# Seven products in place of eight: the MLP matrices of a hybrid diffusion step by Strassen's scheme

## The chip, the cores and the metric

The kernel runs on one core of a Trainium2 chip. The metric is the time of one execution on the device in microseconds, as the median of several runs; lower is better. On the core, TensorE (PE) multiplies, VectorE (DVE), ScalarE (ACT) and GpSimd (POOL) work elementwise, and SyncE (SP) issues the transfers (DMA) between DRAM and the core's memory.

## The reference

One inference step of a backbone of two layers, with 128 context tokens and 1024 latent tokens of width 1024. Layer 0 mixes the tokens with a gated linear recurrence in both directions, layer 1 with multi-head latent attention. Each mixer is followed by an MLP; both stand behind an RMS norm with a shift and a scale and ahead of a gate, and these six vectors of a layer come from a condition vector by a matrix (adaLN):

```python
def sq_relu_mlp(h, w1, w2):
    a = jax.nn.relu(h @ w1)          # 1024 -> 4096
    return (a * a) @ w2              # 4096 -> 1024
...
    for l in range(DEPTH):           # DEPTH = 2
        sh1, sc1, g1, sh2, sc2, g2 = adaln_params(cond, ada_w[l], ada_b[l])
        h = modulate(rms_norm(x, norm_mix[l]), sh1, sc1)
        x = x + g1[:, None, :] * mixer(h)
        h = modulate(rms_norm(x, norm_mlp[l]), sh2, sc2)
        x = x + g2[:, None, :] * sq_relu_mlp(h, mlp_w1[l], mlp_w2[l])
```

## The kernel before

**Layout.** The 1152 tokens (latent ones first) are the columns of every tile, cut into three chunks of 384 columns; the 1024 features are eight blocks of 128 partitions. X, the residual stream, is three tiles of 128 × 8 × 384 in f32.

**Products.** Each operand is split into a high part (a cast on ACT) and a low part (a subtraction, `split`, L137). `mm3` (L119) multiplies them with three matmuls of 128 × 128 by 384 columns, high by high, high by low and low by high (L121, L124, L125). So a block of 128 outputs over 1024 inner rows and one chunk is 24 matmuls.

**Weights.** They come as a stream of pieces of 128 × 1024, 512 KB each, in the order of their use. `prefetch` (L83) loads the next piece into one of two `raw` buffers (SP), makes the high part on ACT (L94) and the low part on GpSimd (L96; on VectorE in the recurrent stage), three or four pieces ahead of the one in use. After each piece it calls `ada` (L150), as often as `ada_rate` says: an adaLN job loads 128 rows of the adaLN matrix into the same two `raw` buffers and takes two dots of 128 × 1024 on VectorE (`ada_dot`, L143), one for each condition. In MLP 0 there is one job for each piece; all jobs of layer 1 are done there.

**The MLP** (`mlp`, L346) goes through eight groups of 512 of the 4096 inner rows. Up: four blocks, each over all three chunks, with relu and square on ACT (L353, L354) and the split on ACT and VectorE. Down: eight blocks of the output over these 512 rows, each over three chunks; the result goes from PSUM with the gate into X on VectorE (`residual`, L298). Nothing of the hidden values leaves the core. Each MLP has 4,608 matmuls.

**Around it.** `out_proj` (L696) is the product behind the mixer, eight blocks over the three chunks in two halves; the norm of a chunk follows in the generator `norm_mod` (L269): the sum of squares and the root (`rstd`), then PE spreads the result over the partitions (`spread`, L260), then VectorE and ACT scale, shift and split (`modulate`, L276: L284 scales, L288 makes the high part, L289 the low part). `tick` and `later` set at which point of PE's work each step is written. Instructions of each engine run in the order in which the scheduler of the language puts them, which starts from the order of the code; each waits for the data and buffers it needs.

Of the kernel before, what the change touches and what calls it, by code (L numbers as in the profile page):

```python
# [15 lines left out]
D = 1024  # L16
# [34 lines left out]
RG_STREAM = list(dict.fromkeys((_k, _n // 2 * 2 if _k == "g" else _n) for _k, _n, *_ in RG_ORDER))  # L51
ADA_ORDER = [(0, 5)] + [(1, _j) for _j in range(6)]
# [3 lines left out]
class Emit:  # L56
    def __init__(self, nc, tc, ins, outs):
# [6 lines left out]
        self.cap = 1 << 30  # L64
        self.ready = []
# [17 lines left out]
    def prefetch(self, upto):  # L83
# [3 lines left out]
        while self.piece_i < min(upto, self.cap, self.I["wts"].shape[0]):  # L87
            raw = self.wp.tile([128, 1024], F32, tag="raw", name="raw", bufs=2)
            nc.sync.dma_start(raw, self.I["wts"][self.piece_i])
            extra = self.wpx is not None and self.piece_i % 4 == 3  # L90
            pool, n = (self.wpx, 1) if extra else (self.wp, 3)
            hi = pool.tile([128, 1024], F32R, tag="whi", name="whi", bufs=n)
            lo = pool.tile([128, 1024], F32R, tag="wlo", name="wlo", bufs=n)
            nc.scalar.copy(out=hi, in_=raw)  # L94
            eng = nc.vector if self.piece_i < len(RG_STREAM) else nc.gpsimd
            eng.tensor_tensor(out=lo, in0=raw, in1=hi.bitcast(F32), op=ALU.subtract)  # L96
            self.ready.append((hi, lo))
# [4 lines left out]
            self.ada(n)  # L102

# [15 lines left out]
    def mm3(self, ps, w, h, first, last):  # L119
        nc = self.nc  # L120
        mm = nc.tensor.matmul(ps, lhsT=w[0], rhs=h[0], start=first, stop=False)  # L121
        if first and self.pin:
            self.tc.keep_in_program_order(mm)
        nc.tensor.matmul(ps, lhsT=w[0], rhs=h[1], start=False, stop=False)  # L124
        nc.tensor.matmul(ps, lhsT=w[1], rhs=h[0], start=False, stop=last)  # L125
# [143 lines left out]
    def norm_mod(self, c, x, st, l, js, hi, lo):  # L269
        nc = self.nc  # L270
        yield 4.0
        y = self.rstd(st, D)
        yield 5.0
        self.modulate(c, x, self.spread(y), l, js, hi, lo)

    def modulate(self, c, x, r, l, js, hi, lo, ks=range(KT)):  # L276
        for k in ks:
            for a, b, cond in segs(c):
                t = self.cell()[:, :b - a]
                self.scale_part(t, x[:, k, a:b], r[:, a:b], self.mod[:, l, js + 1, cond, k:k + 1])  # L280
                self.shift_part(t, hi[:, k, a:b], lo[:, k, a:b], self.mod[:, l, js, cond, k:k + 1])
# [11 lines left out]
    def cbig(self, dt, name):  # L293
        return self.cpool.tile([128, 8, CH], dt, tag="C", name=name)
# [9 lines left out]
    def group(self, items, rhs, drain, after=None, chunks=range(NCH)):  # L304

        last = {pi: (m, pi) for m, pi, _ in items}
        for c in chunks:
            self.need(c)
            for m, pi, blocks in items:
# [5 lines left out]
                if c == NCH - 1 and (m, pi) == last[pi]:  # L315
# [26 lines left out]
    def dense(self, p0, ms, rhs, drain, after=None):  # L342
        self.group([(m, p0 + i, range(8)) for i, m in enumerate(ms)], rhs, drain, after)


    def mlp(self, p0, l, H, after_acc, after):  # L346
        nc = self.nc
        for g in range(8):
            hid = [self.cbig(F32R, "hid") for _ in range(NCH)]

            def up(m, c, ps):
                r = self.cell()
                nc.scalar.activation(out=r, in_=ps, func=AF.Relu)  # L353
                nc.scalar.activation(out=r, in_=r, func=AF.Square)  # L354
                self.split(hid[c][:, m], hid[c][:, 4 + m], r)

            def down(m, c, ps):
                self.residual(c, m, ps, l, 5)
                if g == 7:
                    after_acc(c, m)  # L360
# [869 lines left out]
```

## Time and profile before

| what | us |
|---|---|
| median of 3 runs | 2831.04 (2830.58 to 2831.68) |
| the profiled execution | 8126.54 |
| its span | 8124.8 |
| busy in it: PE / VectorE / ACT / GpSimd | 8089.1 / 1430.2 / 1188.1 / 458.2 |
| window of MLP 0 in it, 1455 to 4250 | 2795 |
| window of MLP 1 in it, 6060 to 8125 | 2065 |

The profiled execution took 2.87 times as long as the timed ones, at a granted clock of 1.00. In a row of the costliest groups stand line, engine, operation, the tile written and the tiles read, shapes and count, then the busy time of the group in us, the mean of one in ns, and the engine's idle time ahead of them with what ended it. In a row of a line or tile stand the shortest, the median and the longest in ns. In a row of the windows stand start and end, length, busy time and count of PE, PEld (weight loads), VectorE, ACT and GpSimd, the clock, the share of the transfer engines and GB/s. A row of the timeline has the start, the time it took, the engine and the line.

### The profile page before, as it was taken

What the parts mean: (1) busy time and instruction counts of PE and PEld (TensorE: products, weight loads), DVE (VectorE), ACT (ScalarE), POOL (GpSimd) and SP (SyncE); (2) the same over time, 40 slices, a digit from 0 to 9 for tenths busy, and PEclk for the clock granted to TensorE, in tenths of its full rate; (3) what the DMA queues carried; (4) which work ended last, traced back from release to release, by engine and by line L of the source; (5) the groups of instructions that cost most, each with busy time, mean ns of one, the idle gap of its engine ahead of it and who ended that gap; (6) DMA issues with size and microseconds to landing.
All of it is one profiled execution on the core that took longest, in us unless ns stands there. A gap on an engine that the chain in (4) does not pass through costs nothing.

```text
span 8124.8 us, 39857 instructions
## 1 busy us (share of the span) xinstructions
PE 8089.1 (100%) x16123; PEld 6011.4 (74%) x16123; DVE 1430.2 (18%) x2845; ACT 1188.1 (15%) x2194; POOL 458.2 (6%) x232
## 2 busy tenths in 40 slices
PE   9999999999999999999999999999999999999999
PEld 5565567777777777777777788888877777777777
DVE  3312221211111111110012223322121000110002
ACT  2222210100010000101011123333111110001101
POOL 0000000000000000000001100000000000000000
DMA  2000010000000000000001120000100000000000
GB/s 89 29 18 26 26 42 31 13 21 29 29 23 24 21 21 24 26 29 13 11 18 43 37 67 21 24 18 29 69 16 18 13 21 11 21 15 16 19 13 29
DMA packets 75145, 215.49 MB, mean 27 GB/s; under 512 B 7632, under 2 KB 33040, under 8 KB 73296
## 3 DMA queue, kind: packets, MB, share of 16 engines
q1 hardware_dynamic: 74192, 209.79, 7.6%
q0 software_dynamic: 768, 3.15, 0.1%
q8 instruction: 127, 2.08, 0.1%
q14 instruction: 58, 0.48, 0.0%
HBM read 181.80 MB, written 28.48 MB: 26 GB/s over the span
## 4 chain that ended last, share of the span: by engine, by line
PE 100%; DVE 0%; ACT 0%; DMA 0%; issue 0%; SPq 0%; DVEq 0%; ACTq 0%
PE ps L121 28%; PE ps L124 28%; PE ps L125 28%; PE ps L166 3%; PE ps L984 2%; PE ps L928 1%; PE ps L1008 1%; PE ps L1010 1%; PE ps L930 1%; PE ps L931 1%; PE ps L932 1%; PE ps L1009 1%; PE ps L929 1%; PE ps L236 1%; PE ps L910 0%; PE ps L912 0%
## 5 line engine op out<-in xcount | busy, mean ns | idle before, releaser
L121 PE MATMUL ps<-hhi,whi 128*128 128x384 f32 x2088 | 1654.0, 795 | 3.0 <-ACT hhi L288 3.0
L125 PE MATMUL ps<-hhi,wlo 128*128 128x384 f32 x2088 | 1655.4, 793 | 0.0
L124 PE MATMUL ps<-hlo,whi 128*128 128x384 f32 x2088 | 1655.0, 793 | 0.0
L121 PE MATMUL ps<-hid,whi 128*128 128x384 f32 x1536 | 1185.2, 772 | 0.0
L124 PE MATMUL ps<-hid,whi 128*128 128x384 f32 x1536 | 1184.7, 771 | 0.0
L125 PE MATMUL ps<-hid,wlo 128*128 128x384 f32 x1536 | 1184.2, 771 | 0.0
L121 PEld LDWEIGHTS ps<-hhi,whi 128*128 128x128 f32 x2088 | 833.6, 399 | 317.2 <-issue 256.9
L124 PEld LDWEIGHTS ps<-hlo,whi 128*128 128x128 f32 x2088 | 830.8, 398 | 308.1 <-issue 255.3
L125 PEld LDWEIGHTS ps<-hhi,wlo 128*128 128x128 f32 x2088 | 837.6, 401 | 291.0 <-issue 241.0
L96 POOL TENSOR_TENSOR wlo<-raw,whi 128x1024 fp32r<-128x1024 f32 x161 | 392.1, 2435 | 6733.3 <-ACT whi L94 6733.3
L121 PEld LDWEIGHTS ps<-hid,whi 128*128 128x128 f32 x1536 | 601.9, 392 | 200.2 <-issue 166.1
L125 PEld LDWEIGHTS ps<-hid,wlo 128*128 128x128 f32 x1536 | 599.3, 390 | 203.6 <-issue 169.0
L124 PEld LDWEIGHTS ps<-hid,whi 128*128 128x128 f32 x1536 | 598.1, 389 | 200.0 <-issue 165.7
L298 DVE SCALAR_TENSOR_TENSOR X<-ps,mod,X 128x256 f32<-128x256 f32 (+1 forms) x576 | 285.9, 515 | 2577.1 <-PE ps L125 2558.2
L94 ACT CAST whi<-raw 128x1024 fp32r<-128x1024 f32 x181 | 189.0, 1045 | 3028.8 <-PE ps L124 3028.8
L140 DVE TENSOR_TENSOR hid<-cell,hid 128x384 fp32r<-128x384 f32 x192 | 139.3, 727 | 1979.3 <-ACT hid L139 1979.3
L353 ACT ACTIVATE cell<-ps 128x384 f32<-128x384 f32 x192 | 94.0, 490 | 1575.5 <-PE ps L125 1575.5
L984 PE MATMUL ps<-ident,p 128*128 128x128 f32 x584 | 216.1, 534 | 2.3 <-ACT p L969 2.3
L933 DVE TENSOR_REDUCE mx<-ps 128x1 f32<-128x384 f32 (+1 forms) x200 | 109.4, 547 | 424.3 <-PE ps L932 424.1
L928 PE MATMUL ps<-k,q 128*128 128x384 f32 (+1 forms) x200 | 171.9, 861 | 0.0
L121 PE MATMUL ps<-zhi,whi 128*128 128x384 f32 x192 | 171.5, 893 | 0.0
L125 PE MATMUL ps<-zhi,wlo 128*128 128x384 f32 x192 | 170.7, 889 | 0.0
(189 smaller groups left out, 6554.7 us busy)
## 6 DMA issues: line engine op xcount, KB each, us to landing
raw<-wts SPq DMA_DIRECT2D x181, 512.0 KB, 3.3
raw<-ada_wt SPq DMA_DIRECT2D x56, 512.0 KB, 3.3
adaw<-ada_n SPq DMA_DIRECT2D x24, 512.0 KB, 3.3
o_d<-o SPq DMA_DIRECT2D x64, 128.0 KB, 1.7
x<-xt SPq DMA_DIRECT2D x3, 1536.0 KB, 13.7
X<-xt SPq DMA_DIRECT2D x3, 1536.0 KB, 8.6
xmid<-X SPq DMA_DIRECT2D x3, 1536.0 KB, 5.7
qn_d<-qn SPq DMA_DIRECT2D x6, 768.0 KB, 3.9
```

What stands on the lines that cost most here:

```text
L94: nc.scalar.copy(out=hi, in_=raw)
L96: eng.tensor_tensor(out=lo, in0=raw, in1=hi.bitcast(F32), op=ALU.subtract)
L121: mm = nc.tensor.matmul(ps, lhsT=w[0], rhs=h[0], start=first, stop=False)
L124: nc.tensor.matmul(ps, lhsT=w[0], rhs=h[1], start=False, stop=False)
L125: nc.tensor.matmul(ps, lhsT=w[1], rhs=h[0], start=False, stop=last)
L140: (lo_eng or nc.vector).tensor_tensor(out=lo, in0=src, in1=hi.bitcast(F32), op=ALU.subtract)
L166: self.nc.tensor.matmul(ps[i][0:2], lhsT=self.cs[:, :, k], rhs=w[:, i * 512:(i + 1) * 512], start=(k == 0), stop=(k == 7))
L298: self.nc.vector.scalar_tensor_tensor(out=self.X[c][:, m, a:b], in0=ps[:, a:b], scalar=self.mod[:, l, j, cond, m:m + 1], in1=self.X[c][:, ...
L353: nc.scalar.activation(out=r, in_=ps, func=AF.Relu)
L928: nc.tensor.matmul(ps, lhsT=qh, rhs=kh[:, a:b], start=True, stop=False)
L933: nc.vector.tensor_reduce(out=mx[:, j:j + 1], in_=ps, axis=AX.X, op=ALU.max)
L984: nc.tensor.transpose(ps[:, j * 128:(j + 1) * 128], p[:, (t * 3 + j) * 128:(t * 3 + j + 1) * 128], self.ident)
```

## The change

In both MLPs the products over chunks 0 and 1 follow Strassen's scheme in the form with few sums. The two chunks are the two column halves of the activations and the two halves of the inner rows their row halves (A11, A12 of chunk 0, A21, A22 of chunk 1); blocks m and m + 2 of the output are the two halves of the weights. In place of eight products of a quarter there are seven, and sums of quarters on both sides. Chunk 2 is multiplied as before. The three matmuls of each product stay. Two up blocks over chunks 0 and 1 had 8 × 12 = 96 matmuls and have 7 × 12 = 84; over chunk 2 they keep 48, of which 24 stand in the pair (108) and 24 in a filler, below. An MLP has 4,224 in place of 4,608.

- **Order of the MLP.** Up and down are no longer interleaved by groups: the whole up matrix comes first, then the whole down matrix. The hidden values of 4096 rows don't fit in the core, so they go to DRAM (`hid_d`, nine tiles of 128 × 2 × 384 per group, sums of quarters among them) and come back.
- **Output product and sums.** The second half of `out_proj` takes the chunks in the order 2, 0, 1. X goes to DRAM (`xs_d`), `modulate` with `keep` writes the modulated values of chunks 0 and 1 over X as well, without the split of the first four blocks of chunk 1, which no product uses. `sums` makes S1 to S4 in place on VectorE, each 1536 columns wide, and splits them.
- **Filler.** 16 of the 32 up blocks over chunk 2 are plain pieces of 24 matmuls: `filler(0, 8)` stands between the output product and the up loop, `filler(8, 8)` between up and down loop.
- **Up loop.** 16 pairs. `prep` loads both weight blocks of the next pair into tiles that lie where X was, splits R0 and half of R1 (low part on GpSimd in layer 0, on VectorE in layer 1), makes four sums of 512 columns and splits the two results on VectorE. The products of a pair give h11, h12, h22 and, in `tail`, h21; sums in `st` cells go to DRAM (`put`). Each pair calls `ada` with two or three jobs.
- **Between.** X is loaded again, hidden values are loaded, then comes the second filler with one adaLN job for each piece.
- **Down loop.** 16 steps d of 132 matmuls (84 in the last two): GpSimd makes two splits and four sums of 256 columns for each raw weight, two raw weights a step; nine hidden tiles a group are loaded and split; the results are added to X by `residual`. The last 96 matmuls are chunk 2 over the last group.
- **Pools.** The nine buffers of one pool become six (tag C) and three (tag G).

The core of the diff:

```diff
+    def sums(self, H):
+        q = [self.X[c][:, 4 * i:4 * i + 4] for c in range(2) for i in range(2)]
+        a11, a12, a21, a22 = q
...
+        sub(a22, a21, a22, ALU.add)
+        sub(a21, a11, a21)
+        sub(a11, a22, a11)
+        sub(a12, a12, a11)
+        for i, t in ((1, a11), (0, a22), (2, a21), (3, a12)):
+            self.split(*S[i], t)
...
+        def put(m, slot, t):
+            nc.sync.dma_start(hid_d[m // 4][:, slot, m % 2], t)
...
+        def drain2(m, c, ps):
+            t = self.cell(tag="acc")
+            relu2(t, ps)
+            put(m, 5, t)
...
+        filler(0, 8)
+        for c in range(NCH):
+            self.need(c)
+        self.release(self.xp)
+        self.upx = self.alloc(name="upx", bufs=1, side="right", reuse_waits="tile")
...
+        leng = nc.vector if l else nc.gpsimd
...
+            if part == 0:
+                r = [self.raw(up_row(i), self.upx, 4) for i in (m, m + 2)]
+                W[p] = {"r": r, "R0": self.wsplit(r[0], leng)}
...
+            if part == 1:
+                w["R1"] = self.wsplit(r1[:, b], leng, 512)
+                add(r0[:, a], r1[:, a], r0[:, a], ALU.subtract)
+                add(r1[:, a], r1[:, b], r1[:, a], ALU.subtract)
+                add(r1[:, b], r1[:, b], r0[:, a], ALU.subtract)
+                add(r0[:, b], r0[:, b], r1[:, b], ALU.subtract)
+            else:
+                w["TY"] = self.wsplit(r1, nc.vector)
+                w["TX"] = self.wsplit(r0, nc.vector)
...
+            A = self.bank()
+            self.prod(A, w["R0"], 0, A11, 4, True)
+            s1 = self.cell()
+            nc.scalar.copy(out=s1, in_=A)
...
+            prep(p + 1, 0)
+            B = self.bank()
+            self.prod(B, w["R0"], 4, A12, 4, True)
+            h11 = st()
+            add(h11, B, s1)
+            nc.scalar.activation(out=h11, in_=h11, func=AF.Relu)
+            square(h11)
+            put(m, 1, h11)
...
+            self.ada(3 if p % 2 else 2)
+        tail()
...
+        load(4)
+        for c in range(NCH):
+            x = self.xp.tile([128, 8, CH], F32, tag="X", name="X")
+            nc.sync.dma_start(x, self.xs_d[l][c])
+            self.X.append(x)
+        load(12)
+        self.ada_rate = 1.0
+        filler(8, 8)
+        self.ada_rate = 0.0
+        self.ada(len(self.ada_jobs))
...
+                    b11, b21, b12, b22 = (raw[:, i * 256:(i + 1) * 256] for i in range(4))
+                    sub = lambda out, x, y: nc.gpsimd.tensor_tensor(out=out, in0=x, in1=y, op=ALU.subtract)
+                    sub(b11, b12, b11)
+                    sub(b12, b22, b12)
+                    sub(b22, b22, b11)
+                    sub(b21, b21, b22)
+                V.append(self.wsplit(raw, nc.gpsimd))
...
+            hi, lo = H2[c] = self.hpair2((2, 0, 1).index(c))
+            self.nc.sync.dma_start(self.xs_d[l][c], self.X[c])
...
-        self.dense(pi + 4, range(4, 8), rhs, drain, after)
-        self.ada_rate = 1.0
+        self.dense(pi + 4, range(4, 8), rhs, drain, after, chunks=(2, 0, 1), last_c=1)
```

How the scheduler places this is seen in the order of the engines' instructions. A row has the line, the operation, the tile written and the tiles read, and the shape.

VectorE in MLP 0 before, in the second group: `hid` are hidden values, `raw` adaLN weights, `mod` their results, `X` the residual stream.

```order
L140 TENSOR_TENSOR hid_4751<-cell_5017,hid_4751 128x384
L145 SCALAR_TENSOR_TENSOR junk_2955,mod_73<-raw_5068,cb_2952 128x1024
L145 SCALAR_TENSOR_TENSOR raw_5068,mod_73<-raw_5068,cb_2952 128x1024
L140 TENSOR_TENSOR hid_4751<-cell_5057,hid_4751 128x384
L140 TENSOR_TENSOR hid_4751<-cell_5097,hid_4751 128x384
L145 SCALAR_TENSOR_TENSOR junk_2955,mod_73<-raw_5108,cb_2952 128x1024
L145 SCALAR_TENSOR_TENSOR raw_5108,mod_73<-raw_5108,cb_2952 128x1024
L140 TENSOR_TENSOR hid_4751<-cell_5137,hid_4751 128x384
L298 SCALAR_TENSOR_TENSOR X_2962<-ps_5152,mod_73,X_2962 128x384
```

VectorE in the up loop of MLP 0 now, in the second pair: `raw_4468` and `raw_4470` are the weights of the next pair, the other `raw` are adaLN weights, `st` the hidden values, `wlo` the low parts of the weight sums.

```order
L170 SCALAR_TENSOR_TENSOR junk_2955,mod_73<-raw_4978,cb_2952 128x1024
L170 SCALAR_TENSOR_TENSOR raw_4978,mod_73<-raw_4978,cb_2952 128x1024
L170 SCALAR_TENSOR_TENSOR junk_2955,mod_73<-raw_4982,cb_2952 128x1024
L170 SCALAR_TENSOR_TENSOR raw_4982,mod_73<-raw_4982,cb_2952 128x1024
L446 TENSOR_TENSOR raw_4470<-raw_4470,raw_4468 128x512
L446 TENSOR_TENSOR raw_4468<-raw_4468,raw_4470 128x512
L446 TENSOR_TENSOR st_4572<-ps_4427,cell_4534 128x384
L170 SCALAR_TENSOR_TENSOR junk_2955,mod_73<-raw_5161,cb_2952 128x1024
L165 TENSOR_TENSOR wlo_4595<-raw_4470,whi_4594 128x1024
L446 TENSOR_TENSOR st_4589<-ps_4521,cell_4519 128x384
L165 TENSOR_TENSOR wlo_4599<-raw_4468,whi_4598 128x1024
L170 SCALAR_TENSOR_TENSOR raw_5161,mod_73<-raw_5161,cb_2952 128x1024
```

The dots stood one job to a piece, which is 72 matmuls of PE; now, in pairs 1 to 8, four jobs, eight dots, stand in a pair of 108, among the sums and splits that PE waits for. The code asks for two or three jobs a pair; the scheduler puts them this early, and in pairs 9 to 15 there are none.

SP in MLP 0 before, with pieces and adaLN weights by turns:

```order
L89 DMA raw_5022<-wts 128x1024
L154 DMA raw_5028<-ada_wt 128x1024
L89 DMA raw_5062<-wts 128x1024
L154 DMA raw_5068<-ada_wt 128x1024
L89 DMA raw_5102<-wts 128x1024
```

SP now at the start of MLP 0: `acc` are results of the filler on their way to DRAM, `raw_4246` and `raw_4248` the first up weights.

```order
L415 DMA hid0_2<-acc_4180 128x384
L415 DMA hid0_3<-acc_4209 128x384
L179 DMA raw_4602<-ada_wt 128x1024
L415 DMA hid0_3<-acc_4238 128x384
L111 DMA raw_4246<-wts 128x1024
L111 DMA raw_4248<-wts 128x1024
```

The first up weights are issued behind the store of the filler's last result; their tile lies where X was.

SP now between the two matrices of MLP 0: `acc_7309` is the first result of the second filler, `raw_7313` the third of its eight weights.

```order
L415 DMA hid0_4<-acc_7309 128x384
L563 DMA X_7250<-xs0 128x3072
L563 DMA X_7252<-xs0 128x3072
L563 DMA X_7254<-xs0 128x3072
L111 DMA raw_7313<-wts 128x1024
L179 DMA raw_7319<-ada_wt 128x1024
L415 DMA hid0_4<-acc_7368 128x384
L111 DMA raw_7323<-wts 128x1024
L179 DMA raw_7329<-ada_wt 128x1024
L111 DMA raw_7333<-wts 128x1024
```

Weights and adaLN weights go by turns as before, with the three loads of X and the stores of the filler among them, while a piece is now 24 matmuls of PE.

More of the change, by code (lines that the diff above doesn't have):

```diff
@@ L86, in prefetch @@
             upto = min(upto, len(RG_STREAM) + 3)
[L87 to L94, printed above, removed]
+        while self.piece_i < min(upto, self.cap, len(STREAM)):
+            raw = self.raw(STREAM[self.piece_i])
             eng = nc.vector if self.piece_i < len(RG_STREAM) else nc.gpsimd
-            eng.tensor_tensor(out=lo, in0=raw, in1=hi.bitcast(F32), op=ALU.subtract)
-            self.ready.append((hi, lo))
+            self.ready.append(self.wsplit(raw, eng))
             self.piece_i += 1
@@ L102, in prefetch, with raw, wslot, wsplit @@
             self.ada(n)
+    def raw(self, row, pool=None, n=2):
+        t = (pool or self.wp).tile([128, 1024], F32, tag="raw", name="raw", bufs=n)
+        self.nc.sync.dma_start(t, self.I["wts"][row])
+        return t
+    def wslot(self):
+        kind = self.wcycle[self.wi % len(self.wcycle)]
+        self.wi += 1
+        if kind == "c":
+            t = self.cbig(F32R, "wc", "G").rearrange("p a b -> p (a b)")
+            return t[:, :1024], t[:, 1024:2048]
+        pool, n = {"wp": (self.wp, 3), "x": (self.wpx, 1), "u": (self.upx, 1)}[kind]
+        return tuple(pool.tile([128, 1024], F32R, tag=t, name=t, bufs=n) for t in ("whi", "wlo"))
+    def wsplit(self, raw, eng, n=1024):
+        hi, lo = (t[:, :n] for t in self.wslot())
+        self.split(hi, lo, raw, eng)
+        return hi, lo
     def piece(self, i):
@@ L279, in modulate @@
                 t = self.cell()[:, :b - a]
+                sh = self.mod[:, l, js, cond, k:k + 1]
                 self.scale_part(t, x[:, k, a:b], r[:, a:b], self.mod[:, l, js + 1, cond, k:k + 1])
-                self.shift_part(t, hi[:, k, a:b], lo[:, k, a:b], self.mod[:, l, js, cond, k:k + 1])
+                if not (keep and c == 1 and k < 4):
+                    self.shift_part(t, hi[:, k, a:b], lo[:, k, a:b], sh)
+                if keep and c < 2:
+                    self.nc.scalar.activation(out=x[:, k, a:b], in_=t, func=AF.Identity, bias=sh, scale=1.0)
     def scale_part(self, out, x, r, sc):
@@ L291, in shift_part, with cbig, hpair2 @@
         )
-    def cbig(self, dt, name):
-        return self.cpool.tile([128, 8, CH], dt, tag="C", name=name)
+    def cbig(self, dt, name, tag="C"):
+        return self.cpool.tile([128, 8, CH], dt, tag=tag, name=name, bufs=6 if tag == "C" else 3)
+    def hpair2(self, i):
+        return tuple(self.cbig(F32R, n, t) for n, t in zip(("hhi", "hlo"), ("GG", "GC", "CC")[i]))
     def residual(self, c, m, ps, l, j):
@@ L301, in residual, with group @@
             )
-    def group(self, items, rhs, drain, after=None, chunks=range(NCH)):
+    def group(self, items, rhs, drain, after=None, chunks=range(NCH), last_c=NCH - 1):
         last = {pi: (m, pi) for m, pi, _ in items}
@@ L314, in group @@
                 drain(m, c, ps)
[L315 removed]
+                if c == last_c and (m, pi) == last[pi]:
                     self.done(pi)
@@ L340, in need, with dense @@
                 self.advance(e)
-    def dense(self, p0, ms, rhs, drain, after=None):
-        self.group([(m, p0 + i, range(8)) for i, m in enumerate(ms)], rhs, drain, after)
-    def mlp(self, p0, l, H, after_acc, after):
-        nc = self.nc
[L348 to L360, printed above, removed]
-            self.dense(p0, range(4), lambda k, c: (H[c][0][:, k], H[c][1][:, k]), up)
-            p0 += 4
-            self.ada_until(l, 5)
-            self.group(
-                [(m, p0 + m // 2, [(m % 2) * 4 + k for k in range(4)]) for m in range(8)],
-                lambda k, c: (hid[c][:, k], hid[c][:, 4 + k]), down, after if g == 7 else None,
-            )
-            p0 += 4
-        return p0
+    def dense(self, p0, ms, rhs, drain, after=None, **kw):
+        self.group([(m, p0 + i, range(8)) for i, m in enumerate(ms)], rhs, drain, after, **kw)
@@ L697, in out_proj @@
         sts = [{} for _ in range(NCH)]
-        H2 = []
+        H2 = {}
+        self.cap = pi + 16
         def drain(m, c, ps):
             self.residual(c, m, ps, l, j)
-            self.sq_acc(sts[c], self.X[c][:, m], m)
+            for i in range(m + 1) if m == 4 and c < 2 else [m] if m > 4 or c == 2 else []:
+                self.sq_acc(sts[c], self.X[c][:, i], i)
             if l == 0 and m < 4 and c > 0:
```

244 lines of the change are left out of this document (226 added, 18 removed).

## The prediction

> **What bounds the kernel now.** The page's busy times were read first, then the windows of each stage, then the lines and forms of VectorE, GpSimd and the transfers.
>
> ```profile
> span 8124.8 us, 39857 instructions
> PE 8089.1 (100%) x16123; PEld 6011.4 (74%) x16123; DVE 1430.2 (18%) x2845; ACT 1188.1 (15%) x2194; POOL 458.2 (6%) x232
> L353 ACT ACTIVATE cell<-ps 128x384 f32<-128x384 f32 x192 | 94.0, 490 | 1575.5 <-PE ps L125 1575.5
> ```
>
> PE is busy for the whole profiled span; the others are nearly idle, and ACT, before it takes a result of the up product, waits for PE (1575.5 us). The windows are, in turn, the recurrent stage, its output product, MLP 0, attention, its output product and MLP 1; the columns are span, then PE, PEld, DVE, ACT and POOL busy with counts, the clock, DMA share, GB/s:
>
> ```profile
> 0.00:1140.00 1140.00, 1120.94 (x1643) 670.56 (x1644) 308.40 (x441) 256.11 (x363) 13.11 (x12) 1.00 0.10 37
> 1140.00:1455.00 315.00, 315.00 (x517) 226.51 (x516) 51.53 (x86) 20.31 (x30) 20.02 (x10) 1.00 0.10 34
> 1455.00:4250.00 2795.00, 2795.00 (x4622) 2005.41 (x4621) 371.21 (x659) 234.63 (x403) 166.92 (x70) 1.00 0.06 22
> 4250.00:5780.00 1530.00, 1525.47 (x4090) 1278.74 (x4089) 414.37 (x1091) 423.27 (x962) 85.12 (x60) 1.00 0.10 34
> 5780.00:6060.00 280.00, 280.00 (x640) 220.18 (x640) 49.81 (x99) 30.59 (x51) 25.20 (x14) 1.00 0.14 51
> 6060.00:8125.00 2065.00, 2052.65 (x4619) 1610.04 (x4617) 234.92 (x469) 223.17 (x386) 147.81 (x66) 1.00 0.05 17
> ```
>
> The profiled execution took 8126.54 us, 1.7 us more than its span; the timed runs took 2831.04 us, 2.87 times less. PE alone is stretched: the two MLPs have the same matmuls and show 2795 and 2065 us, together more than the timed kernel. So PE durations of this trace can't be used; VectorE, ACT, GpSimd and transfer durations fit into 2831 us as they are. The sum therefore runs against 2831, and every slack of those engines must be measured against a much faster PE than the page shows.
>
> **The price of a matmul.** All matmuls of the MLPs have 384 columns. If all windows shrink alike, the MLPs are (2795 + 2065) / 8126.54 of 2831.04 = 1693 us, over 9,241 records 0.183 us. If the recurrent stage and attention can't go below VectorE and ACT one after the other (308 + 256, 414 + 423 = 1402), the four PE-bound windows share 1429 us over 10,398 records: 0.137. If those two stages go down to their busier engine (308 + 423 = 731), it is 0.202. I take the middle of the ends, 0.17, and keep both. A product of 12 matmuls is then 2.0 us, a pair of up blocks (108) 18.4, a plain piece (24) 4.1, a filler of eight pieces 32.6, a down step (132) 22.4.
>
> **What is removed.** Per MLP 4,608 matmuls become 4,224: 768 fewer in all, **−131 us** (−105 to −155) as long as PE stays fed. Everything else the change does is to feed it.
>
> **Prices of the feeding.**
>
> ```profile
> L96 POOL TENSOR_TENSOR wlo<-raw,whi x161: 2341/2362/3398, 1033.5 to 7971.9; 128x1024 fp32r<-128x1024 f32 x161
> L96 DVE TENSOR_TENSOR wlo<-raw,whi x20: 1216/1225/1227, 21.2 to 1010.1; 128x1024 fp32r<-128x1024 f32 x20
> L140 DVE TENSOR_TENSOR hid<-cell,hid x192: 545/558/1347, 1524.6 to 7977.2; 128x384 fp32r<-128x384 f32 x192
> L298 DVE SCALAR_TENSOR_TENSOR X<-ps,mod,X x576: 334/545/620, 1157.0 to 8108.5; 128x384 f32<-128x384 f32 x94, 128x128 f32<-128x128 f32 x50, 128x256 f32<-128x256 f32 x48
> L145 DVE SCALAR_TENSOR_TENSOR junk<-raw,cb x56: 1211/1217/3316, 1216.6 to 3647.8; 128x1024 bf16<-128x1024 f32 x56
> L145 DVE DVE_READ_ACCUMULATOR raw<-raw,cb x56: 76/82/85, 1219.0 to 3660.9; 128x1 f32 x56
> L284 DVE SCALAR_TENSOR_TENSOR cell<-X,mod,ps 128x384 f32<-128x384 f32 x48 | 27.6, 605 | 21.4 <-PE ps L264 21.2
> L289 DVE SCALAR_TENSOR_TENSOR hlo<-cell,mod,hhi 128x384 fp32r<-128x384 f32 x64 | 44.8, 738 | 45.9 <-ACT hhi L288 45.9
> L562 DVE SCALAR_TENSOR_TENSOR ti<-ti,xf 128x1152 f32<-128x1152 f32 x16 | 21.7, 1357 | 176.2 <-ACT ti L552 176.2
> L94 ACT CAST whi<-raw 128x1024 fp32r<-128x1024 f32 x181 | 189.0, 1045 | 3028.8 <-PE ps L124 3028.8
> L354 ACT ACTIVATE cell<-cell 128x384 f32<-128x384 f32 x192 | 100.3, 523 | 5.8
> L228 POOL TENSOR_TENSOR acc<-acc,cell x33: 992/1002/2377, 10.4 to 8099.0; 128x384 f32<-128x384 f32 x33
> raw<-wts SPq DMA_DIRECT2D x181, 512.0 KB, 3.3
> 1131.65 0.33 SPq L89 DMA_DIRECT2D raw<-wts  x1
> 1132.50 11.08 SPq L374 DMA_DIRECT2D X<-xt  x3
> ```
>
> VectorE takes 558 ns for 384 columns and 1357 for 1152, some 1.04 ns a column: 0.69 us for 512 columns, 1.75 for 1536. A weight is at hand 0.33 + 3.3 + 1.05 + 2.36 = 7.0 us after its buffer came free: issue, transfer, ACT, GpSimd.
>
> **Start of each MLP, +36.** The first up weights lie on the place of the old X, so their transfer waits for the last split of the operand sums. The spread of chunk 1's norm stands behind five filler pieces on PE (20.4), then come the modulation (8 × 0.605 + 4 × 0.738 + 0.6 of ACT = 8.4), four sums and four splits of 1536 (8 × 1.75 = 14.0), in layer 0 two dots among them (2.4), then the weight, 7.0: 52.2 against the filler's 32.6, so PE waits 19.6. In layer 1 there are no dots and VectorE makes the low half (1.23): 16.
>
> **Up loop, +33 in layer 0, 0 in layer 1.** Each pair asks VectorE for four weight sums (2.8), two splits (2.45), three sums out of PSUM (1.6), four of SBUF (2.2) and, in eight pairs of layer 0 where the order packs the adaLN dots, eight dots at 1.30 (10.4): 19.5 us against PE's 18.4. Two rows of the timeline bear on it:
>
> ```profile
> 1680.07 2.91 POOL L96 TENSOR_TENSOR wlo<-raw,whi 128x1024 fp32r<-128x1024 f32 x1 [14.58 <-ACT whi L94]
> 1680.81 3.25 DVE L145 SCALAR_TENSOR_TENSOR raw<-raw,cb 128x1024 f32<-128x1024 f32 x1
> ```
>
> A dot that takes 1.22 alone took 3.25 and ended 1.1 us after GpSimd's split: it stood still while that ran. The residual, out of PSUM, never exceeds 0.62. In layer 0 GpSimd makes 2.36 + 1.3 us of splits per pair, now beside a VectorE that is never idle: up to 23.2 a pair. Over eight pairs (19.5 to 23.2 − 18.4) × 8 = 9 to 38; I take 22.5 a pair, since only the PSUM sums fit beside GpSimd: 33. The Trainium skill ("SBUF — State Buffer", Who interferes with whom) states this as a rule, one exclusive lock for the port pair of VectorE and GpSimd; the trace agrees (3.25 us for 1.22), and by it the term is 38, without it 9. In layer 1, with no dots and GpSimd's splits on VectorE (1.9), it has 11 us of work per pair, so nothing.
>
> **Between the matrices, +61.** SP is one queue. In layer 0 the reload of X (three transfers that hold SP for 11.1 us) stands behind the store of the filler's first result (PE 4.1, ACT 0.49 + 0.52, issue 0.33) and ahead of the third filler weight: ready at 5.4 + 11.1 + 6.7 = 23.2 us, due at 8.2. Then each weight waits until GpSimd has finished the one before, since the adaLN weights hold the other raw buffer: 7.0 apiece against 4.1. The eighth is ready at 23.2 + 5 × 7.0 = 58.2 and done at 62.3, against 32.6: 30. The first down weight stands behind the last two dots (2.6), loses some 9, its second half behind four GpSimd sums (1.00 for 384 and 2.36 for 1024, so 0.73 for 256) and two splits some 7 more: 46. In layer 1 nothing but X and the store delays the third weight: 15 (23.2 − 8.2).
>
> **Down phase, +8** (0 to 30). At 14 group boundaries the loads of hidden values wait for PE to free a tile, 0.6 each. In a step of 22.4 us GpSimd has four splits and eight sums (4 × 2.36 + 8 × 0.73 = 15.3), VectorE 18 residuals (9.8) and 4.5 splits of 768 columns (0.96 each), so 14, 17 with small ones: both are covered. If that cover goes, every microsecond costs 32 over both layers.
>
> **At nothing:** eight new stores a pair and nine loads in two steps (SP 0.33 us each), since the windows show 0.05 to 0.10 of the transfer engines busy; ACT, with 13 cell passes (6.6) and 3.5 weight casts (3.7) in a pair of 18.4; the chunk order 2, 0, 1 of the output product, which moves work among stretches where PE has all it needs; the three stores of X a layer, ahead of the filler's on SP but behind no load that is due; the last norm, which follows chunk 2's last matmul as before. If SP or ACT lose that cover, a pair shows it on PE at once, 32 times.
>
> Sum: −131 + 36 + 33 + 61 + 8 = +7, so 2838 us. The ends are wide: the gain alone moves by 26 and 24, and the stalls move against it, as a slower PE hides more.
>
> The Trainium skill ("TensorE: Matmul & The Clock Gate", What's actually happening) has the array at half clock after an idle window of some 3.4 us, for as long again; every row above shows clock 1.00, and no run here has such a gap. By an estimate from that page, six gaps would add about 10 us, to 2848.
>
> **Rivals.**
> - *PE is slower than I price it* (0.20 a matmul, near the upper end). The gain is then 154, a pair takes 21.6 and hides most of VectorE's 22.5 (7 left of 33), the start costs 17 + 14 = 31, the middle 25 + 16 + 14 = 55, boundaries 8: −154 + 101 = −53, 2778 us. For it: the page has PE at 100%, and shrinking all windows alike gives 0.183. Against it: the recurrent stage has little PE work, so its window should shrink less. It decides from about 0.174 on, where the terms cancel.
> - *The lock costs little*, as VectorE falls back on PSUM sums and GpSimd runs in its gaps: up loop 9 in place of 33, 2814 us. For it: the split in the row lost 0.55 itself (2.91 against 2.36), so VectorE got part of its work done beside it. Against it: the next dot stood for the rest, and VectorE now leaves no gaps there.
> - *GpSimd becomes the bound of the down phase.* Its 12 instructions a step have 7.1 us of slack; if each waits 0.75 us for VectorE (a 384-wide one takes 0.56, a 768-wide 0.96), a step takes 15.3 + 9 = 24.3, 32 steps lose 1.9 each: 2838 + 61 = 2899 us. It decides from 0.6 us each. For it: the sum of 992 ns once took 2377. Against it: half of VectorE's work there comes out of PSUM.
>
> **How the numbers follow.** A measurement of this kernel tells about 0.2%, 5.7 us, from no change. Forecast, 2805 to 2880 around 2838: 0.42, of it 0.09 faster, 0.08 same, 0.25 slower. Slow PE, around 2778: 0.19. Little lock, around 2814: 0.16, of it 0.12 faster, 0.04 same. GpSimd, around 2899 and above: 0.19. Unforeseen waits: 0.04 slower. Faster 0.40, same 0.12, slower 0.48. The range leaves out the far third of the slow-PE case (0.06), the upper half of the GpSimd case and what is unforeseen (0.14): 2755 to 2900; the likeliest case alone spans 2805 to 2880.
>
> **What the next profile shows.** Right, if 768 matmuls are gone, if PE idles 16 to 20 us before the first pair of each MLP on the weight sums' chain, if VectorE is busy without a gap through eight pairs of MLP 0 with dots of 2 to 3 us, and if the filler between the matrices waits for weights in MLP 0 more than in MLP 1. If PE is as stretched there as here, these gaps shrink in the profile and only the timed runs and single changes can tell. Wrong, if the time falls below 2755 (the stalls are not there, or a matmul costs 0.2), or if steps of the down phase wait for GpSimd or hidden values.

## The result and the profile after

The changed kernel took 3056.95 us (median of 4 runs, 3054.89 to 3061.66) against 2830.81 before: a ratio of 1.0802 (95% interval 1.0783 to 1.0820). The side was right, slower, and the size was not: 226 us lost where 7 were forecast, outside the range of 2755 to 2900.

The profile of the changed kernel is not stretched, and another profiled execution of the kernel before (the first experiment) is not either, so PE can be read in both. The page of the changed kernel:

```profile
span 3059.9 us, 40925 instructions
PE 2716.5 (89%) x15355; PEld 2619.7 (86%) x15355; DVE 1934.0 (63%) x3445; ACT 1376.1 (45%) x2442; POOL 860.9 (28%) x560
```

768 records of PE are gone, and PE is idle for 343 us of the span; in the second profile of the kernel before it is idle for 84. The windows below cut the MLPs of the changed kernel by counting matmuls: first filler (192), up loop (1,728), second filler (192), down loop (2,112), for MLP 0 and then for MLP 1; a gap between two stages counts to the later one. The column behind POOL's count is the granted clock, then come the share of the transfer engines and GB/s.

```profile
478.40:523.80 45.40, 38.90 (x211) 37.78 (x210) 37.62 (x72) 28.86 (x55) 15.14 (x7) 0.89 0.44 139
523.80:863.20 339.40, 310.54 (x1730) 304.86 (x1729) 262.97 (x368) 161.89 (x281) 69.61 (x34) 0.96 0.58 185
863.20:938.30 75.10, 39.55 (x194) 36.15 (x193) 40.17 (x55) 20.66 (x32) 15.83 (x7) 0.80 0.71 241
938.30:1433.90 495.60, 411.63 (x2144) 404.19 (x2144) 287.55 (x461) 132.57 (x158) 292.92 (x205) 0.89 0.30 99
2146.20:2190.60 44.40, 37.62 (x211) 36.68 (x211) 37.90 (x68) 30.18 (x56) 15.10 (x7) 0.92 0.43 138
2190.60:2508.10 317.50, 304.49 (x1731) 303.74 (x1730) 172.53 (x245) 164.17 (x280) 3.04 (x2) 0.98 0.41 137
2508.10:2563.90 55.80, 37.30 (x193) 36.15 (x192) 14.48 (x14) 23.11 (x35) 23.63 (x13) 0.82 0.69 245
2563.90:3045.00 481.10, 405.52 (x2145) 399.44 (x2143) 283.63 (x460) 125.45 (x151) 278.67 (x197) 0.91 0.28 94
```

The two MLPs of the kernel before, in its second profile:

```profile
473.80:1296.60 822.80, 811.76 (x4657) 810.42 (x4656) 383.82 (x698) 242.08 (x415) 160.83 (x71) 1.00 0.23 77
1998.50:2814.10 815.60, 810.66 (x4659) 809.91 (x4657) 249.69 (x483) 231.28 (x400) 152.40 (x67) 1.00 0.13 43
```

In both kernels a matmul of 384 columns starts every 0.173 to 0.175 us when nothing holds it (0.174 is the median over the changed kernel's 12,936). With 0.174 the kernel before has 802 us of matmuls in each MLP and loses 21 and 14. What the changed kernel loses against 0.174 per matmul, by stage, is this:

| stage | MLP 0 | MLP 1 | both | forecast |
|---|---|---|---|---|
| first filler (33.4 of matmuls) | 12 | 11 | 23 | as before |
| up loop (300.7) | 39 | 17 | 56 | 36 + 33 |
| second filler (33.4) | 42 | 22 | 64 | 61 |
| down loop (367.5) | 128 | 114 | 242 | 8 |

The gain is 768 × 0.174 = 134 us. All losses together are 384 against 35 before, so the MLPs are 216 us longer; the other 15 us of the 231 between the spans lie in the stages around them and were not followed up. Three rows of four are near the forecast. The down loop is not.

### The profile page after: what moved, and what is told of

It reads as the page before. It is cut to its first block, busy times and chain, and to the rows that moved or that the text cites. A ratio compares the mean times of both kernels' runs of the same rounds, so it can differ in the third digit from the quotient of the medians.

```text
span 3059.9 us, 40925 instructions
## 1 busy us (share of the span) xinstructions
PE 2716.5 (89%) x15355; PEld 2619.7 (86%) x15355; DVE 1934.0 (63%) x3445; ACT 1376.1 (45%) x2442; POOL 860.9 (28%) x560
## 4 chain that ended last, share of the span: by engine, by line
PE 44%; POOL 7%; issue 6%; DVE 5%; DMA 4%; ACT 2%; SPq 1%; POOLq 0%; DVEq 0%; ACTq 0%
PE ps L146 11%; PE ps L149 11%; PE ps L150 11%; POOL wlo L165 2%; POOL raw L582 2%; DMA hid<-hid 2%; PE ps L1290 2%; POOL wc L165 2%; PE ps L1234 1%; DMA raw<-wts 1%; PE ps L1238 1%; PE ps L1315 1%; PE ps L1237 1%; PE ps L1236 1%; PE ps L1316 1%
## 5 line engine op out<-in xcount | busy, mean ns | idle before, releaser
L332 DVE SCALAR_TENSOR_TENSOR X<-ps,mod,X 128x384 f32<-128x384 f32 (+2 forms) x768 | 392.2, 537 | 395.5 <-PE ps L150 349.9
L146 PE MATMUL ps<-hhi,whi 128*128 128x384 f32 x1576 | 539.3, 344 | 88.6 <-ACT whi L164 71.5
L150 PE MATMUL ps<-hhi,wlo 128*128 128x384 f32 x1576 | 537.7, 341 | 12.3 <-POOL wlo L165 12.3
L149 PE MATMUL ps<-hlo,whi 128*128 128x384 f32 x1576 | 538.0, 342 | 5.5 <-DVE hlo L319 5.5
L146 PEld LDWEIGHTS ps<-hhi,whi 128*128 128x128 f32 x1576 | 301.9, 192 | 104.5 <-ACT whi L164 73.8
L146 PE MATMUL ps<-hid,whi 128*128 128x384 f32 x824 | 294.4, 357 | 72.1 <-DVE X L332 70.1
L150 PEld LDWEIGHTS ps<-hhi,wlo 128*128 128x128 f32 x1576 | 302.3, 192 | 16.5 <-POOL wlo L165 15.8
L149 PEld LDWEIGHTS ps<-hlo,whi 128*128 128x128 f32 x1576 | 302.7, 192 | 11.9 <-DVE hlo L319 6.6
L150 PE MATMUL ps<-hid,wlo 128*128 128x384 f32 x824 | 291.5, 354 | 3.2 <-POOL wlo L165 3.2
L149 PE MATMUL ps<-hid,whi 128*128 128x384 f32 x824 | 291.6, 354 | 0.0
L146 PE MATMUL ps<-hid,wc 128*128 128x384 f32 x584 | 209.5, 359 | 74.7 <-DVE X L332 68.0
L146 PEld LDWEIGHTS ps<-hid,whi 128*128 128x128 f32 x824 | 167.1, 203 | 77.5 <-DVE X L332 44.0
L150 PE MATMUL ps<-hid,wc 128*128 128x384 f32 x584 | 206.0, 353 | 1.1 <-POOL wc L165 1.1
L149 PE MATMUL ps<-hid,wc 128*128 128x384 f32 x584 | 206.6, 354 | 0.0
```

The lines of the kernel that those rows point to most:

```text
L332: self.nc.vector.scalar_tensor_tensor(out=self.X[c][:, m, a:b], in0=ps[:, a:b], scalar=self.mod[:, l, j, cond, m:m + 1], in1=self.X[c][:, ...
```

## The down loop: what PE waits for there

Who waited for whom in the down loop of MLP 0 of the changed kernel (in total, times, longest), first PE, then SP:

```profile
PE ps L146 <- DVE X L332: 68.3, 15, 6.9
```
```profile
SPq L111 <- POOL wlo L165: 212.0, 24, 21.3
SPq L111 <- POOL wc L165: 155.4, 14, 19.3
SPq L555 <- PE ps L150: 58.7, 23, 12.8
```

PE waits for VectorE's residuals (L332), 4.6 us at a time in the mean, though VectorE is busy for only 288 of the 496 us. SP stands for 367 of 496 us ahead of weight loads (L111), until GpSimd has made the last split of an earlier weight and so freed its buffer. The loads of the hidden tiles (L555) are in the same queue. One such wait, from the timeline of the changed kernel (start, duration, engine, line):

```profile
1099.35 10.65 SPq L111 DMA_DIRECT2D raw<-wts  x2
...
1107.25 2.40 POOL L165 TENSOR_TENSOR wlo<-raw,whi 128x1024 fp32r<-128x1024 f32 x1
...
1110.11 0.85 SPq L555 DMA_DIRECT2D hid<-hid  x2
1114.38 1.70 ACT L164 CAST hid<-hid 128x768 fp32r<-128x768 f32 x2 [8.37 <-DMA hid<-hid]
1115.24 0.96 DVE L165 TENSOR_TENSOR hid<-hid 128x768 fp32r<-128x768 f32 x1 [5.13 <-ACT hid L164]
1116.12 0.61 DVE L332 SCALAR_TENSOR_TENSOR X<-ps,mod,X 128x384 f32<-128x384 f32 x1
1116.78 0.69 PE L146 MATMUL ps<-hid,whi 128*128 128x384 f32 x1 [3.17 <-DVE X L332]
1117.27 0.52 PE L149 MATMUL ps<-hid,whi 128*128 128x384 f32 x1
1117.59 0.52 PE L150 MATMUL ps<-hid,wlo 128*128 128x384 f32 x1
...
1119.83 0.41 PE L146 MATMUL ps<-hid,wc 128*128 128x384 f32 x1
1120.08 0.34 PE L149 MATMUL ps<-hid,wc 128*128 128x384 f32 x1
1120.25 0.33 PE L150 MATMUL ps<-hid,wc 128*128 128x384 f32 x1
```

SP sits on the second weight load until GpSimd's split ends (1109.65). Only then go two hidden tiles out (1110.11). ACT casts them 4.3 us later, VectorE, which takes its instructions in order, has stood 5.1 us at their low part, and the residual behind it comes at 1116.12. That residual frees the bank that PE adds to next. Then PE's own rows: behind the gap a matmul starts every 0.32 us (1117.27, 1117.59) for some 3 us, and every 0.17 after that (1120.08, 1120.25). The windows view of the slow stretch has a granted clock of 0.50 (behind the counts):

```profile
1116.78:1119.80 3.02, 3.02 (x9) 3.02 (x10) 3.02 (x6) 0.00 (x0) 0.00 (x0) 0.50 0.00 0
```

So each gap costs itself and a second stretch at half clock.

## The experiments

The theory (A) was this queue: hidden loads stand on SP behind weight loads that wait for GpSimd. Its main rival (B) was the prediction's own: GpSimd is too slow for a step of the down loop. A third (C): PE frees the hidden tiles too late, whoever loads them. Experiments 1 to 11 are one execution each; executions of the changed kernel differ by up to 7 us and those of experiment 12 by 11, so small differences of the total decide little.

**1. The kernel before, again.** No edit.

> The kernel before, unchanged, for a profile that isn't stretched. In the changed kernel a 384-column matmul starts every 0.174 us at full clock, and 5 to 6% of the matmuls start every 0.32 us right behind a gap. Theory A (the slow matmuls are new, made by the new gaps): the kernel before shows under 10 us of such loss in its two MLPs, and each MLP takes 802 to 820 us. Theory B (they are in every kernel): the loss per MLP is like the changed kernel's, some 35 us. Time 2831 either way.

2831.02 us, windows as shown above: 823 and 816 us at clock 1.00, with 21 and 19 matmuls at half clock in the two MLPs (2.6 and 2.3 us lost), against 75 us in the changed kernel's, 59 of them in the down loops. A of this experiment holds, though MLP 0 is 3 us above the 820 that it named: the half-clock matmuls are new and come from the new gaps.

**2. Down weights loaded from GpSimd's queue.**

```diff
-                    raw = D["raw"] = self.raw(base + (n // 8) * 8 + 4 + n // 2 % 4)
+                    raw = D["raw"] = self.raw(base + (n // 8) * 8 + 4 + n // 2 % 4, eng=nc.gpsimd)
```

> The loads of the down weights are issued by GpSimd in place of SP. Theory A (SP is blocked: hidden loads stand behind weight loads that wait for GpSimd's splits to free a buffer): SP's waits for GpSimd in the down loops go, the hidden loads are issued early, PE's gaps in the two down loops fall from 162 us together to under 60 and the slow matmuls behind them from 55 to under 25: 2920 to 2960 us. Theory B (GpSimd itself is too slow for a step): no gain, as GpSimd has the same work and the issues besides: 3050 to 3090. Theory C (the hidden tiles are freed too late by PE): 3020 to 3057.

2989.03 us. The two down loops:

```profile
934.50:1394.90 460.40, 401.01 (x2145) 393.48 (x2144) 294.39 (x458) 132.06 (x157) 313.92 (x237) 0.92 0.33 107
2525.10:2972.00 446.90, 395.98 (x2145) 389.96 (x2143) 294.18 (x460) 126.43 (x153) 299.34 (x227) 0.94 0.31 101
```

35 and 34 us less, while GpSimd is busier than before (314 against 293 us): B falls, since GpSimd did more and the loop went faster. But the time lies between A's range and C's, and the gain is about half of what A expected. The waits of SP and PE in the loop of MLP 0:

```profile
SPq L555 <- PE ps L150: 364.3, 30, 44.0
SPq L111 <- POOL wc L165: 22.6, 2, 14.6
SPq L111 <- POOL wlo L165: 21.3, 6, 7.6
```
```profile
PE ps L146 <- DVE X L332: 39.4, 12, 6.1
```

SP waits 44 us for GpSimd in place of 367, but the hidden loads now wait, one behind the other, for PE to free their tiles (eight of them take SP 19.78 us from 1093.91 on), so a piece of C is in it, and VectorE took 4.74 us for two hidden splits beside GpSimd's (0.96 each alone).

**3. Hidden tiles loaded from ACT's queue.**

```diff
-                nc.sync.dma_start(lo.bitcast(F32), hid_d[i // 9][:, i % 9])
+                nc.scalar.dma_start(lo.bitcast(F32), hid_d[i // 9][:, i % 9])
```

> The loads of the hidden values are issued by ACT in place of SP. Theory A (SP blocked): they no longer stand behind SP's waits for GpSimd, but ACT now waits for PE to free their tiles, with casts behind it; gaps of the down loops from 162 us to 60 to 110: 2950 to 3010 us. Theory B (GpSimd too slow): 3050 or more. Theory C (tiles freed too late): 3040 or more.

2906.46 us, better than any of the three expected. The down loops, and the waits in that of MLP 0:

```profile
933.20:1348.80 415.60, 387.82 (x2144) 383.20 (x2143) 273.45 (x456) 132.80 (x157) 291.61 (x205) 0.95 0.37 117
2484.10:2889.10 405.00, 382.28 (x2145) 378.97 (x2143) 273.21 (x460) 127.54 (x152) 280.87 (x201) 0.97 0.35 111
```
```profile
SPq L111 <- POOL wlo L165: 225.5, 24, 19.3
SPq L111 <- POOL wc L165: 149.7, 14, 13.9
```
```profile
PE ps L146 <- DVE X L332: 13.7, 5, 4.2
```

One word in one line, and the loops lose 80 and 76 us. SP waits for GpSimd as long as ever (375 us), and now no hidden load is behind it; PE's wait for the residuals falls from 68.3 to 13.7. With experiment 2 this shows A: the place in the queue held the loads back. It does not show that A alone is worth the 80 us, for with this edit the scheduler also places VectorE's hidden splits otherwise. Of the 60 in MLP 0's loop, 20 follow directly on another one in the changed kernel, 16 in experiment 2 and 6 here, so that fewer residuals stand behind two of them. No run parts the two.

**4. The four GpSimd sums left out.**

```diff
-                    sub(b11, b12, b11)
-                    sub(b12, b22, b12)
-                    sub(b22, b22, b11)
-                    sub(b21, b21, b22)
```

> The four sums of down weights on GpSimd are left out (256 instructions of 0.74 us in all, so the down products use wrong weights). Theory A (SP blocked behind GpSimd): a weight buffer comes free 2.9 us earlier, 5.9 us a step of 30 us; part of the gaps goes: 2960 to 3010 us. Theory B (GpSimd too slow): its work a step falls from 15.3 to 9.4 us and nearly all gaps of the down loops go: 2860 to 2920. Theory C (tiles freed too late): 3040 or more.

2953.33 us; 7 us under A's range and 33 above B's. The down loops took 443.9 and 431.1 us, 52 and 50 less: GpSimd lost some 110 us of work in each (183 and 167 busy) and PE got less than half of it back. B falls here too: if GpSimd's work bounded the loop, nearly all of it would have come back.

The remaining runs go on from the third, one stall at a time.

**5. The first pair's weights in the ordinary buffers.**

```diff
-                r = [self.raw(up_row(i), self.upx, 4) for i in (m, m + 2)]
+                r = [self.raw(up_row(i), *((self.upx, 4) if p else ())) for i in (m, m + 2)]
```

> On top of the third experiment (2906 us): the first pair's two weights of each up loop are loaded into the two ordinary raw buffers, not into the tiles that lie where X was. Theory A (they wait for the operand sums, which hold X's place): PE's gaps of 15.9 and 13.0 us ahead of the up loops fall under 6 each, with the half-clock matmuls behind them: 2878 to 2890 us. Theory B (the operands S1 to S4 come too late as well, or the ordinary buffers come free no earlier): 2900 to 2908.

2891.54 us: the up loops go from 338.4 to 333.0 and from 317.6 to 309.1. That is 1.5 us above A's range. PE's wait ahead of the first pair is gone, so it was there for the reason given, but 10 of the 15.7 us come back inside the loop of MLP 0, and 4.5 of the 13.0 in MLP 1, where PE now waits for the weight sums.

**6. The up loop's splits on VectorE in layer 0.**

```diff
-        leng = nc.vector if l else nc.gpsimd
+        leng = nc.vector
```

> On top of the third experiment (2906 us): in layer 0 VectorE, not GpSimd, makes the low parts of R0 and R1 in the up loop. Theory A (GpSimd's split stops VectorE for its whole length): VectorE goes from up to 23.2 us a pair to 21.4 and gains up to 1.8 us in each of eight pairs: 2890 to 2904. Theory B (no such stop): it goes from 19.5 to 21.4 and PE loses 1.9 more in each of eight pairs: 2915 to 2925.

2882.56 us. The up loop of MLP 0 in the third experiment, and here:

```profile
518.10:856.50 338.40, 308.84 (x1729) 302.91 (x1728) 263.25 (x367) 161.94 (x281) 70.89 (x34) 0.97 0.58 185
```
```profile
518.10:838.80 320.70, 304.75 (x1729) 304.01 (x1728) 255.62 (x399) 163.46 (x281) 4.33 (x2) 0.97 0.60 195
```

VectorE took over 32 splits and is busy for 8 us less: beside GpSimd its instructions stand still and count as busy. The loop is 18 us shorter, and beyond the start stall only some 4 us of loss are left in it. A holds, 7 us beyond its range. The second to the eighth pair of the changed kernel, in one window, show what went away:

```profile
563.00:710.00 147.00, 137.00 (x756) 132.72 (x754) 143.75 (x212) 64.09 (x118) 32.79 (x14) 0.99 0.73 224
```

VectorE is busy for 143.75 of 147 us there, and a pair takes 21.0 us; here the same pairs take 18.8 to 18.9.

**7. Three adaLN jobs in every pair, held in place.**

```diff
-            self.ada(3 if p % 2 else 2)
+            self.pin_ada = True
+            self.ada(3)
+            self.pin_ada = False
```

(With `pin_ada`, the load and the dots are kept behind what is written ahead of them on their engine.)

> On top of the third experiment (2906 us): three adaLN jobs in each of the 16 pairs of MLP 0, held at their place in the order, in place of four in eight pairs and the rest in the second filler. Theory A (the packed dots overload VectorE, and adaLN weights slow the filler): PE's 16 us of gaps inside the up loop fall under 6, and the second filler of MLP 0 loses what that of MLP 1 loses (43 to 25): 2872 to 2884. Theory B (the gaps come from ACT's copies of PSUM and the filler's from the hidden values): 2898 to 2910.

2887.05 us, 3 above A's range and 11 under B's, and by another way than expected. The up loop got longer (348.9 against 338.4), the second filler of MLP 0 shorter (61.6 against 76.7) and its down loop too (402.9 against 415.6, now like that of MLP 1). So the adaLN weights did hold up the filler and the first down weights, as forecast; the packed dots were not what the up loop lost to, GpSimd's splits beside them were (experiment 6).

**8. Hidden tiles cast between the filler's pieces.** The loads of X and of the first twelve hidden tiles stay ahead of the second filler on SP.

```diff
-                self.split(hi, lo, lo.bitcast(F32))
...
+                if i >= 12:
+                    self.split(hi, lo, lo.bitcast(F32))
...
-        filler(8, 8)
+        for i in range(8, 16):
+            filler(i, 1)
+            for hi, lo in [D[j] for j in range(2 * i - 20, 2 * i - 18) if j >= 0]:
+                self.tc.keep_in_program_order(nc.scalar.copy(out=hi, in_=lo.bitcast(F32)))
```

> On top of the third experiment (2906 us): the first twelve hidden tiles are still loaded ahead of the second filler (by SP, like X), but ACT casts them between the filler's pieces, not ahead of its first weights. Theory A (ACT, in order, waits for hidden tiles from DRAM ahead of the weight casts that PE waits for): the 19.7 and 19.5 us gaps at the head of the second fillers go: 2864 to 2880. Theory B (the prediction's: the reload of X on SP delays the third weight): the reload is where it was, so 2900 to 2910.

2904.36 us: B. The timeline of SP ahead of the second filler of MLP 1, and PE's first matmul behind the gap:

```profile
2436.27 1.59 SPq L565 DMA_DIRECT2D X<-xs  x3
...
2439.01 1.04 SPq L111 DMA_DIRECT2D raw<-wts  x2
...
2455.52 0.69 PE L146 MATMUL ps<-hhi,whi 128*128 128x384 f32 x1 [15.04 <-ACT whi L164]
```

X's loads hold SP for 1.59 us, not 11; but the weights issued 2.7 us behind them are cast at 2454.43, 15 us after their issue where a weight takes 3.7 otherwise. In that wait the transfer engines are full, at 416 GB/s and a share of 1.01 (a packet counts whole where it starts):

```profile
2439.00:2454.50 15.50, 1.48 (x9) 1.16 (x7) 0.00 (x0) 1.09 (x3) 0.00 (x0) 0.72 1.01 416
```

So the weights stand behind X and the hidden tiles in the transfers, not in the queue of instructions.

**9. Three fixes together**: experiments 3, 5 and 6, and `self.ada(3)` for each pair without holding it in place, so that no adaLN job is left for the filler.

> Hidden loads on ACT's queue, the first pair's weights in the ordinary buffers, the up loop's splits on VectorE in layer 0, and three adaLN jobs called for in each pair (placed by the scheduler), so that none is left for the second filler. Theory A (the stalls add up): 2906 less 15 (start) less 24 (splits) less some 15 (filler of MLP 0 without adaLN weights) = 2850 us, 2840 to 2860. Theory B (the dots now overload VectorE: 9.1 + 1.9 + 7.8 = 18.8 against PE's 18.8 a pair): 2865 to 2885.

2843.01 us, as A has it; the up loops take 309.2 and 309.1 us, 8 above their matmuls.

**10 and 11. The reloads behind the filler's weights.** In the tenth, X is loaded ahead of the filler's fourth piece; in the eleventh, only four hidden tiles come first, eight more ahead of the third piece and X ahead of the fifth (one piece further back, not two as its text says). From the eleventh:

```diff
         load(4)
...
+        for i in range(8, 16):
+            if i == 10:
+                load(12)
+            if i == 12:
+                for c in range(NCH):
...
+                    self.tc.keep_in_program_order(nc.sync.dma_start(x, self.xs_d[l][c]))
```

> The ninth experiment, and between the matrices the reload of X is issued behind the weights of the filler's first three pieces, not ahead of all but two; the twelve hidden tiles stay ahead of the filler, cast between its pieces. Theory A (the weights wait for X's 4.5 MB on the transfer engines, ahead of them in SP's order): the gap of 15 to 20 us at the head of each second filler goes, less what X then makes late: 20 to 30 us less than the ninth. Theory B (the hidden tiles, 4.5 MB as well, hold the weights back alone): under 8 us less.

> The tenth, with eight of the twelve hidden tiles issued behind the weights of the filler's first pieces too, and X two pieces further back. Theory A (X alone was in the way): like the tenth within 8 us, or slower by up to 15 as X and hidden tiles now come late for the down loop. Theory B (the hidden tiles are in the way): 10 to 25 us less than the tenth.

2835.13 and 2823.60 us: 7.9 less, then 11.5 less. By the totals B holds in both, so the 4.5 MB of hidden tiles were in the way as well as the 4.5 MB of X. By stage it is less clear. The two second fillers together go from 120.9 us in the ninth to 108.0 and 87.7, but the two down loops from 807.8 to 811.2 and 826.8: of the 20 us that the eleventh gains in the fillers, 16 come back behind them, as its A warned, and only 5 of its 11.5 us lie in these four stages. The second fillers of the eleventh:

```profile
826.40:875.80 49.40, 39.20 (x194) 37.82 (x193) 21.97 (x28) 21.42 (x32) 14.89 (x6) 0.86 0.86 304
2356.00:2394.30 38.30, 35.56 (x194) 34.90 (x192) 17.99 (x14) 21.10 (x32) 15.18 (x6) 0.96 0.94 349
```

That is 75.1 and 55.8 us in the changed kernel against 49.4 and 38.3 here, with the transfer engines at 0.86 and 0.94. Beyond their matmuls (33.4 us) these two stages have 16 and 5 us left to gain.

**12. The first three raw down weights on VectorE.**

```diff
+                eng = nc.vector if n < 6 else nc.gpsimd
...
-                V.append(self.wsplit(raw, nc.gpsimd))
+                V.append(self.wsplit(raw, eng))
```

> The eleventh, and the first three raw down weights of each MLP are summed and split by VectorE, which idles there, in place of GpSimd (some 16 us less on GpSimd's chain at the head of each down loop). Theory A (PE's gaps of 2 to 4 us at the head of each down loop, 11 us a layer, are GpSimd's chain of split, four sums and split): 5 to 9 us less a layer: 2806 to 2816 us. Theory B (VectorE and GpSimd stop each other there, or the weights' transfers are the last to come): 2820 to 2828. Against the kernel before (2831): faster by 0.5 to 0.9% by A, 0.1 to 0.4% by B.

2805.11 us (median of 5) against 2831.49: a ratio of 0.9916 (95% interval 0.9901 to 0.9930), so 0.8% less than the kernel before. A holds, a microsecond beyond its range: the MLPs take 9 and 8 us less than in the eleventh. The two MLPs, all four stages in one window for each:

```profile
469.30:1277.60 808.30, 764.86 (x4274) 757.61 (x4273) 615.92 (x1002) 343.72 (x525) 303.72 (x202) 0.97 0.52 169
1989.80:2786.60 796.80, 759.34 (x4275) 753.24 (x4273) 510.48 (x803) 342.97 (x520) 295.57 (x198) 0.98 0.42 136
```

So of the 67 us that the removed matmuls are worth in each MLP, 14 and 19 are left as a gain when the largest stalls are gone; the down loops of this version still lose 37 and 40 us.

## Why the prediction was wrong, point by point

- **The price of a matmul, 0.17 us (0.137 to 0.202): right.** It is 0.174, and the gain is 134 us where 131 were forecast.
- **Start of each MLP, +36: right, a little high.** PE waits 15.7 and 13.0 us for the first weight (29), for the reason given; experiment 5 takes that wait away, and 14 of the 29 us are gained.
- **Up loop, +33 in layer 0 and 0 in layer 1: right in kind, high in size.** MLP 0 loses 39 − 16 = 23 in the loop, MLP 1 some 4. The row of one dot beside one split carried it: VectorE is without a gap through these pairs, as forecast (143.75 of 147 us), and experiment 6 shows GpSimd's split stopping it, and that the stop, not the sum of VectorE's work, is what the loop lost to.
- **Between the matrices, +61: the size came out (64), in part by luck, for one mechanism was wrong.** X's loads don't hold SP for 11 us, they take 1.6 to 1.9. The row of 11.08 us covers three issues and the waits between them; each issue in it took 0.33 to 0.42. What the loads hold is the transfer engines, together with the hidden tiles, which the sum did not count (experiments 8, 10, 11). The adaLN part held (experiment 7).
- **Down phase, +8 (0 to 30): this is the step that failed.** It put the loads of hidden tiles at "0.6 each" behind PE, and GpSimd's 15.3 us and VectorE's 14 to 17 us in a step of 22.4 as "both are covered". Busy times say nothing of order. SP issued the hidden loads behind weight loads that waited for GpSimd to free one of two raw buffers, and that wait ended when GpSimd was done, not when PE was in need. The loss was 242 us, of which 156 go when the hidden loads leave that queue (experiment 3, the new order on VectorE included). The prediction worked from SP's order between the matrices; it has nothing on SP's order in the down loop.
- **The side, slower: luck.** Without what the down loops lost beyond the forecast (242 − 8) the kernel would have taken some 2823 us by this estimate, less than the kernel before.
- **The rival "GpSimd becomes the bound of the down phase" was not what happened**, though its side was: GpSimd did more work in less time in experiment 2, and less than half of its sums' time came back in experiment 4. The rivals of a slower PE and of a lock that costs little were both wrong.
- **The clock.** The forecast had no term for it. The changed kernel's MLPs lose 75 us to matmuls at 0.32 us behind gaps, the MLPs before 5. The estimate that stood beside the sum, six gaps and 10 us, counted only the gaps that the sum had; the down loops made 32 more. The Trainium skill ("TensorE: Matmul & The Clock Gate", HAM oscillation — how this bites in real kernels) describes this, a wait in each tile that costs a stretch at half clock each time; the trace agrees, with 1.6 us per gap here. The Trainium skill speaks there of gaps above some 3.4 us, as the prediction did; here gaps from 2.2 us on did it, and the measurement decides. The clock of 1.00 in every row of the prediction was that of the stretched profile; the second profile of the same kernel has 0.99.

What stays open: the 15 us outside the MLPs; the share of VectorE's new order in what experiment 3 gained; and the rest in the down loops of the last version. Its predecessor's trace shows a hidden load issued by ACT behind a weight cast that waited 7 us for GpSimd's sums, and PE waiting 4 us for it; that was not tried.

## What to carry to other kernels

Fewer matmuls on a kernel that PE bounds are worth their full price only if nothing new lies ahead of PE, and here most of the stalls could be worked out beforehand, so read the order of every queue that the change fills, in each of its loops, and ask of each waiting issue what stands behind it. A load that a later stage needs on time does not belong in a queue behind a load that waits for a buffer; moving one such line gave more (156 us in the down loops, 150 in all) than the algebra did (134). Where several megabytes come back from DRAM at a change of stage, price them as transfers, in bytes ahead of the next weight, and not as instructions.

## What the runs showed of the hardware

- Half clock starts after short gaps. In the two down loops of the changed kernel 32 gaps of 2.2 to 7.8 us were followed by 1 to 18 matmuls at 0.32 us each (10.6 in the mean, so 1.6 us lost a gap). Gaps near 2.3 us did it as well as gaps of 6, with 4 to 11 such matmuls behind them. In the trace's records of the clock the stretch of 0.50 lasts 3.41 us or a multiple of it, mostly one or two, however long the gap was.
- An engine can look busier for doing less: VectorE's busy time in the up loop fell from 263.25 to 255.62 us when it took 32 splits over from GpSimd, since an instruction that stands still beside a GpSimd split counts as busy.
- Transfers reached 416 GB/s over 15.5 us in experiment 8, with the transfer engines full, and 349 GB/s at 0.94 of them over 38 us in experiment 11, where the kernel before has a mean of 43 to 77 in its MLPs.
- The profile of the kernel before that the prediction used had PE alone stretched, to a span of 8124.8 us; a second one of the same kernel has 2829.3. The prices of the other engines' instructions taken from the first held: GpSimd's split of 1024 columns, 2.36 us there, has a median of 2.40 in the changed kernel, and VectorE's dot has 1.22 in both.
